# A layer's small product, p times w_pp, moved from the last phases to the start and kept in DRAM between

## The chip, the cores and the metric

One core of one Trainium2 chip runs the whole layer. The metric is the time of one execution in microseconds on the device; the median of three runs stands for the kernel. Matmuls run on TensorE (PE), elementwise work on VectorE (DVE), ScalarE (ACT) and GpSimd (POOL); SyncE (SP) issues most DMAs. Each engine works through its own queue in order.

## The reference, cut to what matters

1024 tokens (x: 1024 x 2048), p: 1024 x 256, all float32. The layer's last part is what the change touches:

```python
u = rmsnorm(h, g_pre)                 # h = x
z = u @ w_in                          # 2048 -> 9216: attention and HGRN2 inputs
...
h = h + rmsnorm(y @ w_out, g_post)    # y: 1024 x 2048
gate = sigmoid(h @ w_pg)              # w_pg: 2048 x 2048
e = p_l @ w_pp                        # p_l: 1024 x 256, w_pp: 256 x 2048
h = h + rmsnorm(gate * e, g_ple)
```

The product e depends on the inputs p and w_pp alone; it is needed first where the gate is ready.

## The kernel before

Every large product is made with float32 operands split in two. K.piece (lines 73 to 87) loads a piece of weights of 128 x 512 (256 KB) on SP into one of three raw buffers, ScalarE casts it to the high part wh (line 83), GpSimd subtracts to the rest wl (line 84), VectorE casts a bfloat16 copy wb (line 85); each of the three has three buffers. A bank of PSUM (128 tokens x 512 columns) takes from each piece three matmuls: high x wh, high x wl, low x wb. So a piece that serves four token tiles feeds 12 matmuls. Four banks are called gb, four others wk. Pieces have a high priority by default, which places their instructions ahead of other ready ones; the order on every engine's queue is fixed ahead, by a planner that works with priorities and program order.

The start: prenorm (line 156) loads x in 8 tiles of 1 MB into five buffers, squares and sums each on ScalarE, scales it on VectorE (line 168), transposes it by 16 small matmuls (tile xp, line 172), and splits it into uh and ul by ScalarE and VectorE (lines 151, 152). Between the tiles lies the first column group of the values, v_group (lines 771 to 786): for token tiles 0 and 1, then 2 and 3, then 4 to 7 (accumulators vb from tile 4 on); its pieces have no high priority, and VectorE makes every other subtract where a piece serves only two token tiles. After that come three more column groups for all tokens, the HGRN2 heads, the attention heads.

The end: y_phase makes y @ w_out for a half of the tokens (512) in four column groups of 512, 16 pieces each; g_phase (line 977) does the same with w_pg and in its sink takes the sigmoid on ScalarE, multiplies it into G (which holds e), squares and sums, and multiplies by the gain. The order is y_phase of half 0, y_phase of half 1, g_phase of half 0, g_phase of half 1; hooks between the pieces do other halves' norms (h_unit, with loads xr of x) and the last additions (final0, with loads hr of hD). G of half 0 lies in the buffer of Y[0], G of half 1 in that of the high part of the first half's h.

The product e in this kernel: e_load loads p of a half, e_unit transposes and splits it (hooks of the phase before), and e_phase (line 971) makes one column group of 512 in two pieces of w_pp, into four banks of wk named pe, and copies each bank into G by ScalarE or VectorE. g_phase calls e_phase twice ahead of column group 0 and twice ahead of group 1. The loop gemm (line 874) runs over the pieces; the last tail pieces are kept until all are there and then worked off token tile by token tile, each followed by its sink.

Of the kernel before, what the change touches and what calls it, by code (L numbers as in the profile page):

```python
# [12 lines left out]
F32 = mybir.dt.float32  # L13
F32R = mybir.dt.float32r
BF16 = mybir.dt.bfloat16
# [8 lines left out]
D = 2048  # L24
INW = 9216
KT = 16
NEG = -1e30
EPS = 1e-6
PLE = 256
NGB = 4  # L30
# [7 lines left out]
def f32(t):  # L38
    return t.bitcast(F32)
# [707 lines left out]
def tile_hybrid(ctx, tc, x, p, positions, w_in, w_out, g_pre, g_post, g_hg, lb_fwd, lb_bwd, w_pg, w_pp, g_ple, out):  # L747
    nc = tc.nc
    K = Kern(tc, ctx)
    x2 = x[0]  # L750
    out2 = out[0]
    w_in = w_in[0]
    w_out = w_out[0]
    w_pg = w_pg[0]
    w_pp = w_pp[0]
    pin = p[0, 0]
# [10 lines left out]
    V = nc.vector  # L767
    vD = [K.dr.tile([S, 512], F32, name=f"vD{i}") for i in range(4)]

    def v_group(cg, toks, pool):  # L770
# [12 lines left out]
        for t in toks:  # L783
            vo = pool.tile([128, 512], F32, name="vo", tag="vo", bufs=3)
            (nc.scalar.copy if t % 2 else V.tensor_copy)(vo, pb[t])
            nc.sync.dma_start(vD[cg][128 * t:128 * t + 128, :], vo)

    with tc.tile_pool(name="p0", bufs=1) as p0:
        warm = K.sp.tile([128, 1], F32, name="warm", bufs=1)
        V.memset(warm, 1.0)  # L790
        nc.scalar.activation(warm, warm, AF.Sqrt)
        K.prenorm(x2, g_pre, p0, (0, 1))
        v_group(0, (0, 1), p0)
        K.prenorm(x2, g_pre, p0, (2, 3))
        v_group(0, (2, 3), p0)
        late = K.prenorm(x2, g_pre, p0, (4, 5, 6, 7))
        v_group(0, (4, 5, 6, 7), p0)
        with tc.issue_after(late[0].ins), tc.issue_after(late[1].ins):
            K.hg_consts((lb_fwd, lb_bwd), g_hg)
        for cg in range(1, 4):  # L800
            v_group(cg, tuple(range(8)), p0)
    with tc.tile_pool(name="big", bufs=1) as big:
# [15 lines left out]
        for n, a in enumerate(heads):  # L818
# [13 lines left out]
            if b:  # L832
# [3 lines left out]
                k = b.keys()  # L836
# [6 lines left out]
    fin = ctx.enter_context(tc.tile_pool(name="fin", bufs=1))  # L843
    Y = [fin.tile([128, 4, D], F32, name=f"Y{i}", tag=f"Y{i}") for i in range(2)]
# [4 lines left out]
    def s2(name):  # L849
        return fin.tile([128, 512], F32, name=name, tag="s2", bufs=3)  # L850
# [3 lines left out]
        nc.sync.dma_start(t, src[0:1, cs].to_broadcast([128, 512]))  # L854
        return t

    def chunk(q):
        return slice(512 * q, 512 * q + 512)
# [7 lines left out]
    def y_load(hf, k):  # L866
        hi, lo = yT[hf]
        with tc.high_priority(offset=PRIO):
# [5 lines left out]
    def gemm(w, act, order, c0, sink, tail, bank, pre=None, get=None):  # L874
        toks = range(4)
        hi, lo = act
        pb = [bank() for t in toks]
        n = len(order)
        pcs = []

        def high(t, k, pc, first):
            a = hi[:, k, 128 * t:128 * t + 128]
            nc.tensor.matmul(pb[t], a, pc[0], start=first, stop=False)  # L883
            nc.tensor.matmul(pb[t], a, pc[1], start=False, stop=False)  # L884

        def low(t, k, pc, last):
            nc.tensor.matmul(pb[t], lo[:, k, 128 * t:128 * t + 128], pc[2], start=False, stop=last)  # L887

        for j, k in enumerate(order):
            if pre:  # L890
                pre(j, k)
            pc = K.piece(w[128 * k:128 * k + 128, c0:c0 + 512], [512], get(j) if get else None)
            if j < n - tail:
                for t in toks:
                    high(t, k, pc, j == 0)
                for t in toks:
                    low(t, k, pc, False)
            else:
                pcs.append((k, pc))
        for t in toks:  # L900
            for i, (k, pc) in enumerate(pcs):
                high(t, k, pc, n == tail and i == 0)
            for i, (k, pc) in enumerate(pcs):
                low(t, k, pc, i == len(pcs) - 1)
            sink(t, pb[t])

    def junk_square(src, acc):
        jk = fin.tile([128, 512], BF16, name="jk", tag="jk", bufs=1)
# [2 lines left out]
    def y_phase(hf, hook):  # L911
        for cg in range(4):
            def sink(t, p):
                dst = Y[hf][:, t, chunk(cg)]
                V.tensor_copy(dst, p)  # L915
                junk_square(dst, yss[hf][:, t, cg:cg + 1])
            gemm(w_out, yT[hf], korder, 512 * cg, sink, 1, K.gb, lambda j, k: hook(cg, j, k))
# [37 lines left out]
        if new:  # L955
            pend.append(new)

    eT = {}

    def e_load(hf, dst):  # L960
        tc.keep_in_program_order(nc.sync.dma_start(dst, pin[512 * hf:512 * hf + 512, :].rearrange("(t p) c -> p t c", p=128)))
        eT[hf] = (dst, fin.tile([128, 2, 512], F32R, name="eh", tag="eh"), fin.tile([128, 2, 512], BF16, name="el", tag="el"))

    def e_unit(hf, t):
        src, eh, el = eT[hf]
        pp = K.wk("pp", (128, 2, 128))
        for k in range(2):
            nc.tensor.transpose(pp[:, k], src[:, t, 128 * k:128 * k + 128], K.ident)
        K.split_evac(eh[:, :, 128 * t:128 * t + 128], el[:, :, 128 * t:128 * t + 128], pp)

    def e_phase(hf, G, cg):
        def sink(t, p):
            (V.tensor_copy if t % 2 else nc.scalar.copy)(G[:, t, chunk(cg)], p)
        gemm(w_pp, eT[hf][1:], [0, 1], 512 * cg, sink, 1, lambda: K.wk("pe"))

    def g_phase(hf, G, hook, fin_t=None, get=None, tail=1):
        for cg in range(4):
            if cg < 2:
                e_phase(hf, G, 2 * cg)
                e_phase(hf, G, 2 * cg + 1)  # L980
            cs = chunk(cg)
# [29 lines left out]
    hT = [half_tiles("t", 0), None]  # L1011
    r0_ = h_rstd(0)

    def every3(f, ext={}, off=0):
        def hook(cg, j, k=None):
            n = 16 * cg + j
            if n % 3 == off and n // 3 < 17:
                f(n // 3)
            if n in ext:
                ext[n]()  # L1020
        return hook

    def e_hooks(hf, dst, n0, n1):
        ext = {n1 + t: (lambda t=t: e_unit(hf, t)) for t in range(4)}
        ext[n0] = lambda: e_load(hf, dst)
        return ext

    y_phase(1, every3(lambda u: h_unit(0, u, r0_), e_hooks(0, Y[1][:, :, 1536:1792], 16, 52)))
    hT[1] = half_tiles("t", 1)
    r1_ = h_rstd(1)  # L1030
    G0 = Y[0]
    ex = f32(hT[1][1][:, 12:16])
# [68 lines left out]
```

## Time and profile before

| | us |
|---|---|
| median of 3 runs | 2865.4 |
| lowest and highest | 2862.57 and 2868.63 |
| the profiled execution, its own time | 2864.4 |
| its span, first to last instruction | 2862.6 |
| TensorE busy | 2733.1 (95%) |
| VectorE busy | 1433.7 (50%) |
| ScalarE busy | 949.0 (33%) |
| GpSimd busy | 1045.1 (37%) |

Busy time is an average over the whole span; what holds the kernel in a stage is read from the stretches, the waits and the timeline of that stage. A matmul's duration in a row covers its pipeline, so consecutive rows overlap; the distance between starts is its cost.

### The profile page before, as it was taken

Reading aid. Unit: us, or ns where it says so; the run is one execution under the profiler, and the core shown is the slowest. Engines: PE = TensorE matmul, PEld = TensorE weight load, DVE = VectorE, ACT = ScalarE, POOL = GpSimd, SP = SyncE. Lnnn points to the kernel's source line nnn. Section 1 sums busy time; section 2 is a strip of 40 time slices with the busy share of each in tenths; the row PEclk is TensorE's granted clock in tenths of the full one; section 3 lists DMA queues with packets and bytes.
Section 4 is the critical chain, followed back from the end, with each engine's and each line's share of the span. In section 5 each row is a group of like instructions: output and inputs, shape, how many; then the busy total and the mean of one; then the engine's idle time right before and its main releaser. Section 6 shows DMA issues by size and latency. Waiting matters only on the chain. (4 is left out here: it accounts for less than half of the span.)

```text
span 2862.6 us, 45162 instructions
## 1 busy us (share of the span) xinstructions
PE 2733.1 (95%) x17104; PEld 1891.4 (66%) x17104; DVE 1433.7 (50%) x3105; ACT 949.0 (33%) x1996; POOL 1045.1 (37%) x833
## 2 busy tenths in 40 slices
PE   6999999999999999999999999999999899999997
PEld 4666666766766766766677667766666566666664
DVE  8601116765365355353655455545655536545445
ACT  5311112222122122122555444545633233333323
POOL 3422223313313313313222232323244554666555
PEclk9999999999999999999999999999999999999998
DMA  6422221211111111114323433343444543443553
GB/s 229 116 65 78 77 85 42 62 54 38 59 45 46 56 45 49 53 41 104 96 81 89 113 86 80 94 107 91 131 132 135 156 144 99 126 122 107 145 151 114
DMA packets 272218, 267.75 MB, mean 94 GB/s; under 512 B 22784, under 2 KB 187648, under 8 KB 270848
## 3 DMA queue, kind: packets, MB, share of 16 engines
q1 hardware_dynamic: 262832, 255.92, 31.0%
q10 hardware_dynamic: 9168, 8.93, 0.9%
q8 instruction: 135, 2.21, 0.3%
q14 instruction: 83, 0.68, 0.1%
HBM read 208.16 MB, written 29.36 MB: 83 GB/s over the span
## 5 line engine op out<-in xcount | busy, mean ns | idle before, releaser
L84 POOL TENSOR_TENSOR wl<-raw,wh 128x512 fp32r<-128x512 f32 x568 | 767.8, 1356 | 1502.9 <-ACT wh L83 1441.2
L85 DVE CAST wb<-raw 128x512 bf16<-128x512 f32 x584 | 401.8, 692 | 806.9 <-PE gb L107 300.0
L83 ACT CAST wh<-raw 128x512 fp32r<-128x512 f32 x584 | 358.4, 617 | 1243.0 <-PE gb L102 395.3
L102 PE MATMUL gb<-uh,wh 128*128 128x512 f32 x1792 | 739.2, 412 | 0.0
L103 PE MATMUL gb<-uh,wl 128*128 128x512 f32 x1792 | 705.4, 394 | 0.0
L107 PE MATMUL gb<-ul,wb 128*128 128x512 bf16 x1792 | 440.0, 383 | 0.0
L102 PEld LDWEIGHTS gb<-uh,wh 128*128 128x128 f32 x1792 | 337.8, 189 | 83.9 <-issue 2.5
L103 PEld LDWEIGHTS gb<-uh,wl 128*128 128x128 f32 x1792 | 337.3, 188 | 68.3
L107 PEld LDWEIGHTS <-wb 128*128 128x128 bf16 x1792 | 156.6, 98 | 205.3 <-issue 54.8
L883 PE MATMUL gb<-wh,yh 128*128 128x512 f32 x512 | 230.6, 450 | 3.9 <-DVE Y L915 3.2
L883 PE MATMUL gb<-wh,th 128*128 128x512 f32 x480 | 214.5, 447 | 0.1
L884 PE MATMUL gb<-wl,yh 128*128 128x512 f32 x512 | 203.0, 397 | 4.1 <-POOL wl L84 4.1
L884 PE MATMUL gb<-wl,th 128*128 128x512 f32 x480 | 189.2, 394 | 3.1 <-POOL wl L84 3.1
L887 PE MATMUL gb<-wb,yl 128*128 128x512 bf16 x512 | 139.3, 386 | 0.0
L657 ACT ACTIVATE asm<-asm,aown 128x256 f32<-128x256 f32 x256 | 127.0, 498 | 25.7 <-DVE aown L654 24.8
L887 PE MATMUL gb<-wb,tl 128*128 128x512 bf16 x480 | 129.0, 382 | 0.0
L883 PEld LDWEIGHTS gb<-wh,yh 128*128 128x128 f32 x512 | 97.7, 191 | 34.1 <-issue 3.2
L778 PE MATMUL gb<-wh,uh 128*128 128x512 f32 x256 | 116.6, 462 | 3.0 <-ACT wh L83 3.0
L884 PEld LDWEIGHTS gb<-wl,yh 128*128 128x128 f32 x512 | 97.3, 190 | 23.6 <-POOL wl L84 4.6
L779 PE MATMUL gb<-wl,uh 128*128 128x512 f32 x256 | 102.3, 406 | 7.9 <-POOL wl L84 5.5
L883 PEld LDWEIGHTS gb<-wh,th 128*128 128x128 f32 x480 | 90.7, 189 | 27.3 <-ACT sg L987 2.2
L884 PEld LDWEIGHTS gb<-wl,th 128*128 128x128 f32 x480 | 90.4, 188 | 22.9 <-POOL wl L84 5.4
(284 smaller groups left out, 3635.8 us busy)
## 6 DMA issues: line engine op xcount, KB each, us to landing
raw<-in_w_in_dram SPq DMA_DIRECT2D x320, 256.0 KB
raw<-in_w_out_dram SPq DMA_DIRECT2D x128, 256.0 KB
raw<-in_w_pg_dram SPq DMA_DIRECT2D x128, 256.0 KB
xt<-in_x_dram SPq DMA_DIRECT2D x8, 1024.0 KB
vD<-vo SPq DMA_DIRECT2D x32, 256.0 KB
aqt<-aqh SPq DMA_DIRECT2D x64, 128.0 KB
aqt<-aq SPq DMA_DIRECT2D x64, 128.0 KB
raw<-yD SPq DMA_DIRECT2D x32, 256.0 KB
```

The costliest lines, as they stand in the source:

```text
L83: nc.scalar.copy(wh, raw)
L84: (sub or nc.gpsimd).tensor_tensor(wl, raw, f32(wh), op=ALU.subtract)
L85: nc.vector.tensor_copy(wb, raw)
L102: nc.tensor.matmul(pb[hf], wh[:, k], self.uh[hf][:, kt], start=(kt == 0), stop=False)
L103: nc.tensor.matmul(pb[hf], wl[:, k], self.uh[hf][:, kt], start=False, stop=False)
L107: mm = nc.tensor.matmul(pb[hf], wb[:, k], self.ul[hf][:, kt], start=False, stop=(kt == KT - 1))
L657: nc.scalar.activation(d, d, AF.Exp, scale=-1.0, bias=own[:, 0, loc, h, i:i + 1], accum_out=own[:, 1, loc, h, i:i + 1])
L778: nc.tensor.matmul(pb[t], hi, wh, start=(k == 0), stop=False)
L779: nc.tensor.matmul(pb[t], hi, wl, start=False, stop=False)
L883: nc.tensor.matmul(pb[t], a, pc[0], start=first, stop=False)
L884: nc.tensor.matmul(pb[t], a, pc[1], start=False, stop=False)
L887: nc.tensor.matmul(pb[t], lo[:, k, 128 * t:128 * t + 128], pc[2], start=False, stop=last)
```

## The change

e_product is called for both halves ahead of prenorm. It loads p, transposes and splits it, makes the four column groups with gemm (both pieces kept until the end: tail 2; banks gb in place of wk) and copies each bank into a staging tile eo, which SP stores to a DRAM tile eD. gemm and chunk are moved up unchanged for it. v_group is defined a second time, the same but for its staging tile vo, which now shares four buffers (tag tA) with eo in place of three of its own; four pairs of DRAM tiles, sD, are named and not used. In the last phases, e_unit, e_phase and the hooks that called them are gone; g_phase begins with e_load, four DMAs on SP that load the half's product from eD into G, 512 columns (1 MB) each. Lines of "..." leave out code that is moved or deleted unchanged.

```diff
@@ in tile_hybrid, ahead of the pool p0 @@
+    def chunk(q):
+        return slice(512 * q, 512 * q + 512)
+
+    def gemm(w, act, order, c0, sink, tail, bank, pre=None, get=None):
...
+        for j, k in enumerate(order):
+            if pre:
+                pre(j, k)
+            pc = K.piece(w[128 * k:128 * k + 128, c0:c0 + 512], [512], get(j) if get else None)
+            if j < n - tail:
...
+            else:
+                pcs.append((k, pc))
+        for t in toks:
+            for i, (k, pc) in enumerate(pcs):
+                high(t, k, pc, n == tail and i == 0)
+            for i, (k, pc) in enumerate(pcs):
+                low(t, k, pc, i == len(pcs) - 1)
+            sink(t, pb[t])
+
+    eD = [K.dr.tile([512, D], F32, name=f"eD{i}") for i in range(2)]
+
+    def e_product(hf, pool, stage):
+        src = pool.tile([128, 4, PLE], F32, name="pr", tag="pr", bufs=2)
+        nc.sync.dma_start(src, pin[512 * hf:512 * hf + 512, :].rearrange("(t p) c -> p t c", p=128))
+        eh = pool.tile([128, 2, 512], F32R, name="eh", tag="eh", bufs=1)
+        el = pool.tile([128, 2, 512], BF16, name="el", tag="el", bufs=1)
+        for t in range(4):
+            pp = K.wk("pp", (128, 2, 128))
+            for k in range(2):
+                nc.tensor.transpose(pp[:, k], src[:, t, 128 * k:128 * k + 128], K.ident)
+            K.split_evac(eh[:, :, 128 * t:128 * t + 128], el[:, :, 128 * t:128 * t + 128], pp)
+        for cg in range(4):
+            def sink(t, p):
+                eo = stage.tile([128, 512], F32, name="eo", tag="tA", bufs=4)
+                (V.tensor_copy if t % 2 else nc.scalar.copy)(eo, p)
+                nc.sync.dma_start(eD[hf][128 * t:128 * t + 128, chunk(cg)], eo)
+            gemm(w_pp, (eh, el), [0, 1], 512 * cg, sink, 2, K.gb)
+
+    def v_group(cg, toks, pool):
...
+            vo = pool.tile([128, 512], F32, name="vo", tag="tA", bufs=4)
...
     with tc.tile_pool(name="p0", bufs=1) as p0:
         warm = K.sp.tile([128, 1], F32, name="warm", bufs=1)
         V.memset(warm, 1.0)
         nc.scalar.activation(warm, warm, AF.Sqrt)
+        e_product(0, p0, p0)
+        e_product(1, p0, p0)
         K.prenorm(x2, g_pre, p0, (0, 1))
@@ the last phases @@
-    eT = {}
-
-    def e_load(hf, dst):
...
-    def e_unit(hf, t):
...
-    def e_phase(hf, G, cg):
-        def sink(t, p):
-            (V.tensor_copy if t % 2 else nc.scalar.copy)(G[:, t, chunk(cg)], p)
-        gemm(w_pp, eT[hf][1:], [0, 1], 512 * cg, sink, 1, lambda: K.wk("pe"))
+    def e_load(hf, G):
+        for cg in range(4):
+            nc.sync.dma_start(G[:, :, chunk(cg)], eD[hf][:, chunk(cg)].rearrange("(t p) c -> p t c", p=128))
 
     def g_phase(hf, G, hook, fin_t=None, get=None, tail=1):
+        e_load(hf, G)
         for cg in range(4):
-            if cg < 2:
-                e_phase(hf, G, 2 * cg)
-                e_phase(hf, G, 2 * cg + 1)
             cs = chunk(cg)
...
-    y_phase(1, every3(lambda u: h_unit(0, u, r0_), e_hooks(0, Y[1][:, :, 1536:1792], 16, 52)))
+    y_phase(1, every3(lambda u: h_unit(0, u, r0_)))
...
-    g_phase(0, G0, every3(lambda u: h_unit(1, u, r1_), e_hooks(1, ex, 17, 28), 2))
+    g_phase(0, G0, every3(lambda u: h_unit(1, u, r1_), 2))
```

## Rows read from the trace of the kernel before

**Rows 1.** The page of the kernel before: busy time by engine with its share of the span, then TensorE (PE) and its granted clock in the 40 slices.
```profile
PE 2733.1 (95%) x17104; PEld 1891.4 (66%) x17104; DVE 1433.7 (50%) x3105; ACT 949.0 (33%) x1996; POOL 1045.1 (37%) x833
...
PE   6999999999999999999999999999999899999997
...
PEclk9999999999999999999999999999999999999998
```

**Rows 2.** Stretches of the start (from : to in us, length, then busy us and instructions (x) of each engine, the granted clock of TensorE, the share of the DMA engines, GB/s).
```profile
0.00:97.89 97.89, 69.63 (x321) 44.96 (x321) 79.05 (x139) 55.05 (x94) 33.23 (x28) 0.97 0.61 207
...
100.00:110.00 10.00, 10.00 (x46) 6.76 (x45) 7.61 (x48) 3.98 (x7) 5.01 (x4) 1.00 0.38 63
```

**Rows 3.** Waits of TensorE in the first 130 us: who waited for whom, us in total, times, longest.
```profile
PE xp L172 <- DVE xt L168: 14.5, 3, 11.5
...
PE gb L779 <- POOL wl L84: 5.5, 4, 2.9
...
PE gb L778 <- ACT wh L83: 3.0, 3, 1.3
```

**Rows 4.** Timeline of the first 25 us: start, us, engine, line, operation, and the idle time before it with its releaser.
```profile
0.74 0.39 SPq L160 DMA_DIRECT2D xt<-in_x_dram  x1
...
2.12 1.65 SPq L76 DMA_DIRECT2D raw<-in_w_in_dram  x3
...
3.81 0.95 SPq L160 DMA_DIRECT2D xt<-in_x_dram  x2
...
5.61 1.91 ACT L166 ACTIVATE xj<-xt 128x2048 bf16<-128x2048 f32 x1 [3.38 <-DMA xt<-in_x_dram]
...
11.54 3.65 PE L172 MATMUL xp<-ident,xt 128*128 128x128 f32 x16 [11.54 <-DVE xt L168]
...
16.46 0.80 PE L778 MATMUL gb<-wh,uh 128*128 128x512 f32 x1 [1.28 <-ACT wh L83]
...
17.79 2.49 SPq L76 DMA_DIRECT2D raw<-in_w_in_dram  x3
...
22.57 1.94 PE L172 MATMUL xp<-ident,xt 128*128 128x128 f32 x16 [1.23 <-DVE xm L118]
```

**Rows 5.** Timeline of TensorE around the four blocks of the product of p (tile pe); gb rows are the gate product behind a block.
```profile
2414.99 0.59 PE L883 MATMUL pe<-wh,eh 128*128 128x512 f32 x1
...
2427.76 0.58 PE L883 MATMUL gb<-wh,th 128*128 128x512 f32 x1
...
2430.49 0.58 PE L883 MATMUL gb<-wh,th 128*128 128x512 f32 x1
...
2475.86 0.58 PE L883 MATMUL pe<-wh,eh 128*128 128x512 f32 x1
...
2490.95 0.58 PE L883 MATMUL gb<-wh,th 128*128 128x512 f32 x1
...
2632.01 0.59 PE L883 MATMUL pe<-wh,eh 128*128 128x512 f32 x1
...
2643.97 0.50 PE L883 MATMUL pe<-wh,eh 128*128 128x512 f32 x1 [3.17 <-DVE G L973]
...
2648.01 0.58 PE L883 MATMUL gb<-wh,th 128*128 128x512 f32 x1
...
2691.70 0.59 PE L883 MATMUL pe<-wh,eh 128*128 128x512 f32 x1
...
2707.97 0.58 PE L883 MATMUL gb<-wh,th 128*128 128x512 f32 x1
```

**Rows 6.** Instructions on the tiles xp (transposes of x), gb (accumulators, first 140 us) and vb (accumulators of token tiles 4 to 7): duration in ns min/median/max, first and last start.
```profile
L172 PE MATMUL xp<-ident,xt x128: 270/273/444, 11.5 to 97.7; 128*128 128x128 f32 x128
...
L778 PE MATMUL gb<-wh,uh x64: 389/541/988, 16.5 to 90.7; 128*128 128x512 f32 x64
...
L778 PE MATMUL vb<-wh,uh x256: 387/389/586, 97.9 to 398.7; 128*128 128x512 f32 x128
```

**Rows 7.** Groups by line in the first 130 us (busy us, mean ns | idle before), then two casts from the timeline, the second beside a subtract on GpSimd that ran from 55.69 to 57.01 us.
```profile
L84 POOL TENSOR_TENSOR wl<-raw,wh 128x512 fp32r<-128x512 f32 x30 | 46.4, 1553 | 81.2 <-ACT wh L83 62.5 <-PE gb L779 7.0 <-PE gb L782 6.3
...
L85 DVE CAST wb<-raw 128x512 bf16<-128x512 f32 x46 | 30.9, 691 | 14.8 <-PE vb L782 8.3 <-DMA raw<-in_w_in_dram 4.9 <-PE gb L782 1.7
...
L152 DVE TENSOR_TENSOR ul<-xp,uh 128x512 bf16<-128x512 f32 x32 | 20.4, 681 | 2.4 <-ACT uh L151 2.4
...
L168 DVE SCALAR_TENSOR_TENSOR xt<-xt,xr,gpre 128x2048 f32<-128x2048 f32 x8 | 18.8, 2349 | 0.1
...
11.99 0.43 DVE L85 CAST wb<-raw 128x512 bf16<-128x512 f32 x1 [0.25 <-DMA raw<-in_w_in_dram]
...
55.69 1.32 POOL L84 TENSOR_TENSOR wl<-raw,wh 128x512 fp32r<-128x512 f32 x1 [2.55 <-PE gb L782]
...
55.78 1.51 DVE L85 CAST wb<-raw 128x512 bf16<-128x512 f32 x1
```

**Rows 8.** What the DMA engines moved in 40 slices of the first 110 us (2.75 us each); a stretch of the gate phase with a join of two column groups and no product of p in it; one piece of the chain that ended last; the longest wait of ScalarE's cast from 2180 us on.
```profile
GB/s 48 411 426 405 432 423 70 234 268 349 238 255 310 145 154 252 260 196 0 215 136 211 123 259 10 118 182 87 13 162 116 201 143 180 163 168 5 116 85 26
...
2550.00:2600.00 50.00, 49.51 (x228) 32.67 (x227) 27.16 (x32) 18.47 (x35) 36.88 (x28) 1.00 0.42 118
...
2556.00 3.42 DMA xr<-in_x_dram
...
ACT wh L83 <- PE gb L883: 146.9, 85, 8.6
```

More of the change, by code (lines that the diff above doesn't have):

```diff
@@ L786, in v_group, with high, low @@
             nc.sync.dma_start(vD[cg][128 * t:128 * t + 128, :], vo)
+    def chunk(q):
+        return slice(512 * q, 512 * q + 512)
+    def gemm(w, act, order, c0, sink, tail, bank, pre=None, get=None):
+        toks = range(4)
+        hi, lo = act
+        pb = [bank() for t in toks]
+        n = len(order)
+        pcs = []
+        def high(t, k, pc, first):
+            a = hi[:, k, 128 * t:128 * t + 128]
+            nc.tensor.matmul(pb[t], a, pc[0], start=first, stop=False)
+            nc.tensor.matmul(pb[t], a, pc[1], start=False, stop=False)
+        def low(t, k, pc, last):
+            nc.tensor.matmul(pb[t], lo[:, k, 128 * t:128 * t + 128], pc[2], start=False, stop=last)
+        for j, k in enumerate(order):
[4 more added lines that the diff above has]
+                for t in toks:
+                    high(t, k, pc, j == 0)
+                for t in toks:
+                    low(t, k, pc, False)
+            else:
+                pcs.append((k, pc))
+        for t in toks:
+            for i, (k, pc) in enumerate(pcs):
[3 more added lines that the diff above has]
+            sink(t, pb[t])
@@ new lines, in v_group @@
+    def v_group(cg, toks, pool):
+        c0 = (2048, 2560, 7168, 7680)[cg]
+        pb = {t: (K.gb() if t < NGB else K.wk("vb")) for t in toks}
+        for k in range(KT):
+            wh, wl, wb = K.piece(w_in[128 * k:128 * k + 128, c0:c0 + 512], [512], prio=False,
+                                 sub=V if len(toks) == 2 and k % 2 else None)
+            for t in toks:
+                hi = K.uh[t // 4][:, k, 128 * (t % 4):128 * (t % 4) + 128]
+                nc.tensor.matmul(pb[t], hi, wh, start=(k == 0), stop=False)
+                nc.tensor.matmul(pb[t], hi, wl, start=False, stop=False)
+            for t in toks:
+                lo = K.ul[t // 4][:, k, 128 * (t % 4):128 * (t % 4) + 128]
+                nc.tensor.matmul(pb[t], lo, wb, start=False, stop=(k == KT - 1))
+        for t in toks:
+            vo = pool.tile([128, 512], F32, name="vo", tag="tA", bufs=4)
+            (nc.scalar.copy if t % 2 else V.tensor_copy)(vo, pb[t])
+            nc.sync.dma_start(vD[cg][128 * t:128 * t + 128, :], vo)
@@ L788, in tile_hybrid @@
+    sD = [(K.dr.tile([128, 8, 512], F32, name=f"sh{i}"), K.dr.tile([128, 8, 512], BF16, name=f"sl{i}")) for i in range(4)]
     with tc.tile_pool(name="p0", bufs=1) as p0:
@@ L855, in g2 @@
         return t
-    def chunk(q):
-        return slice(512 * q, 512 * q + 512)
     def half_tiles(name, hf):
@@ L872, in y_load @@
             V.tensor_tensor(lo[:, k], raw, f32(hi[:, k]), op=ALU.subtract)
[L874 to L905, printed above, removed]
     def junk_square(src, acc):
@@ L1012, in tile_hybrid, with every3 @@
     r0_ = h_rstd(0)
-    def every3(f, ext={}, off=0):
+    def every3(f, off=0):
         def hook(cg, j, k=None):
@@ L1018, in hook @@
                 f(n // 3)
-            if n in ext:
-                ext[n]()
-        return hook
[L1023 to L1026, printed above, removed]
-    y_phase(1, every3(lambda u: h_unit(0, u, r0_), e_hooks(0, Y[1][:, :, 1536:1792], 16, 52)))
+        return hook
+    y_phase(1, every3(lambda u: h_unit(0, u, r0_)))
     hT[1] = half_tiles("t", 1)
@@ L1031, in tile_hybrid @@
     G0 = Y[0]
-    ex = f32(hT[1][1][:, 12:16])
-    g_phase(0, G0, every3(lambda u: h_unit(1, u, r1_), e_hooks(1, ex, 17, 28), 2))
+    g_phase(0, G0, every3(lambda u: h_unit(1, u, r1_), 2))
     gs = K.sp.tile([128, 4], F32, name="gst4")
```

7 lines of the change are left out of this document (removed).

## Prediction

> **What bounds the kernel now.** I read the page first: TensorE is busy 95% of the span, and only the first and the last of the forty slices fall short of it [rows 1]. So time is won only by taking work off TensorE or by filling its idle time, and the first slice holds much of that. Next, the stretches of the start by window: until 97.9 us TensorE is busy 69.6 us, VectorE 79 us; from 100 us on TensorE has no gap [rows 2]. The waits of TensorE there name VectorE's scaling of x (14.5 us, of which 11.5 ahead of the first instruction) and the weight conversion [rows 3]. The timeline shows the cause: x tile 0, issued at 0.74, is squared from 5.61, TensorE's first transpose comes at 11.54 and its first matmul at 16.46 [rows 4].
>
> **A measure of the start.** A piece of weights feeds 12 matmuls to four banks; undisturbed they take 2430.49 - 2427.76 = 2.73 us [rows 5]. Sixteen transposes take 1.94 us [rows 4]. Up to 97.9 us, where the first matmul into a vb bank starts, TensorE has done 128 transposes and 64 triples, that is 192 matmuls [rows 6]: 8 x 1.94 + 16 x 2.73 = 59.2 us undisturbed. The start thus wastes 97.9 - 59.2 = 38.7 us, 11.5 before the first transpose and 27.2 after it, at half speed or idle.
>
> **What the change removes.** The product of p is made in eight column groups, four to a half of the tokens; they lie in four blocks of two, and nothing else runs on TensorE in them. From a block's first matmul to the first one behind it: 2427.76 - 2414.99 = 12.77, 2490.95 - 2475.86 = 15.09, 2648.01 - 2632.01 = 16.00, 2707.97 - 2691.70 = 16.27 us [rows 5], together 60.1 us. Eight groups of two pieces are 16 x 2.73 = 43.7 us undisturbed, so 16.4 us of the blocks were waits for evacuation and conversion, or half speed. The 16 transposes of p (1.9 us) go too: 62.0 us. Not all of that is won. Part of the waits belongs to the join of two phases (VectorE's chain for the norm and the sigmoid evacuations), and stays without the product. A join without a product inside lies in the stretch from 2550 to 2600 us, with 0.5 us idle [rows 8]; the worst wait in a block is 3.17 us [rows 5]. For four joins that is 2 to 13 us; I take r = 4, nearer to the join that looks like the new ones.
>
> **What it adds at the start.** The same 43.7 + 1.9 = 45.6 us of TensorE, plus what the start wastes then, U. Only U decides whether moving pays. Its terms:
> - First matmul. p is half of an x tile, which took 4.9 us to land [rows 4]; its transposes, split and weight pieces stand behind. Bounds 5 us and today's 11.5; I take 7.5, since VectorE's 2.35 us scaling and the gain row aren't in this path.
> - Half speed. The first matmul of the start takes 0.80 us [rows 4], where 0.39 to 0.58 is usual [rows 5]. Bounds 0 and 4 us; I take 1.5.
> - Eight column groups of two pieces each with three buffers for converted pieces: the second piece of a group waits for a buffer that the previous group frees only with its last bank, then ScalarE, GpSimd (1.55 us here) and VectorE convert [rows 7]. The late blocks had the same ring: (12.77 - 10.92)/2 = 0.9 to (16.27 - 10.92)/2 = 2.7 us a group, mean 2.05. Here both pieces are now held to the end (tail 2), and prenorm's ScalarE and VectorE instructions stand between. Bounds 7 and 32 us; I take the mean, 16.4.
> - The rest of today's 27.2 us. While the product runs (45.6 + 16.4 + 9 = some 71 us), VectorE owes it 16 casts of 0.69, 16 evacuations of some 0.68 (a split of that size) and 8 splits of half the size, 25 us. A prenorm tile costs VectorE 2.35 + 4 x 0.68 + about 1 = 6 us [rows 7], so 46 us remain, up to seven tiles; five x buffers and FIFO order allow some five or six. I leave 8 us; bounds 3 and 27.
> U = 7.5 + 1.5 + 16.4 + 8 = 33 us, against 38.7 now. VectorE's total, 79 + 25 = 104 us, against a stage of 45.6 + 59.2 + 33 = 138, is no bound.
>
> **The queues.** SP now issues two p loads, sixteen w_pp pieces and 32 stores (8.4 MB) ahead of or among the x loads. Each store waits for an evacuation, and x tiles and weight pieces are queued behind it. What waits there: prenorm on ScalarE, hence TensorE's transposes. Today SP put four x tiles, the gain and three pieces into the queue by 4.8 us, and then stood until 17.79 for a free raw buffer [rows 4]. A piece issued at about 3 us behind 3 MB landed at 11.9 [rows 4, 7], so pieces behind x tiles come late. Product, x and gain together are 8.4 + 4.2 + 1.0 + 8.4 + 1.0 = 23 MB; at the first slices' 426 GB/s that is 54 us, at 250 (later slices) 92 us [rows 8], both inside 138 us: covered in sum, and a starved ring is in the bound of 32. GpSimd's 16 subtracts (25 us) lie beside 33 us in 97.9 [rows 2].
>
> **The late loads.** Each half reads its product back in four 1 MB loads on SP. The first half's target is free well before; the second's waits for the last matmul of the first gate phase, and behind it on SP stand w_pg pieces and hr loads. Moving at 118 GB/s with a share of 0.42 is 281 GB/s in full [rows 8], so 4.2 MB in one burst delay a piece behind them by 15 us. The pieces have slack: ScalarE's casts mostly wait for TensorE to free a buffer (146.9 us), so three raw and two converted pieces lie ready, some 4 x 2.73 = 11 us. An xr load already costs 3.42 us of the chain, with GpSimd's subtracts behind it [rows 8]. Bounds 0 and 15 us a half; I take 1 each, L = 2, as SP waits for raw buffers between the loads. The sums of the sink need the first chunk a whole column group later, 16 x 2.73 = 43.7 us: free. Nothing, too, for the DRAM tiles that nobody uses, and for vo's move to four buffers shared with eo: TensorE waits for no vo [rows 3]; should the eo stores land late, evacuations and banks wait for them, which is in the bound of 32.
>
> **Sum.** 45.6 - 62.0 + r + L + (U - 38.7) = U + L + r - 55.1. With 33 + 2 + 4: -16 us. The profiled execution takes 2864.4 us, 1.0 below the median of 2865.4: 2848.4 there, 2849 for the median.
>
> **A rule of the skill.** A cast of 128x512 takes 0.43 us alone and 1.51 us when it meets a subtract on GpSimd [rows 7]. The Trainium skill, "SBUF — State Buffer", section "Who interferes with whom", says that VectorE and GpSimd share one pair of ports as an exclusive lock, the later one blocked for the whole instruction. The trace agrees: that cast ended only after the subtract beside it. It speaks against the change: the sixteen moved pieces come where VectorE is fullest, and by the lock up to 16 x 1.1 = 17 us more would stand in VectorE's queue. This doesn't break the sum (121 of 138 us), but a blocked cast holds up prenorm and evacuation behind it; for it I give rival D 0.10 where I would give 0.05.
>
> **The rivals.**
> - B, better: prenorm hides wholly and a group wastes 0.9 us: U = 7.5 + 1.5 + 7 + 4 = 20, sum -55.1 + 20 + 6 = -29, 2836. For: TensorE no longer waits for x first. Against: the late blocks reached 0.9 only once of four. 0.18.
> - C, it doesn't do what it says: the planner puts prenorm behind the product, so that most of the 27.2 us remain, 24 say, as the x tiles are there by then: U = 7.5 + 1.5 + 16.4 + 24 = 49, sum 0, 2865. For: x loads are now later in program order and w_pp pieces carry the high priority. Against: SP stands idle in the rows and has x buffers free. 0.14.
> - D, slower: the ring of three paces the product, each group waiting behind a 1.91 us square on ScalarE, a 2.35 us scaling on VectorE or a blocked subtract. With j us a group the sum is 9 + 8j + 8 + 6 - 55.1 = 8j - 32: nothing won from j = 4, 5.7 us lost from j = 4.7; at j = 5 it is +8, 2873. For: rows with 3.17 us waits in the late blocks, with less prenorm about. Against: their mean is 2.05. 0.10.
> - E: the read-back comes in bursts and starves pieces, xr or hr: 7 us a half makes -4, 2861; the full 15 makes +12. 0.08.
>
> **How the numbers follow.** The forecast, -24 to -8, has 0.50. Its own range is 2841 to 2857; for 8 in 10 it takes in B (down to 2831), C and the near side of D (up to 2868). A measurement of this kernel can tell some 0.2%, 5.7 us. Faster: 0.50 + 0.18 + 0.05 of C and E = 0.73; within: 0.16, C, half of E, the near side of D; slower: 0.11, D and the ends of C and E.
>
> **What will show it.** The first matmul before 9 us and its operands p and w_pp; groups of the product that take 5.5 us plus about 2; the first vb matmul at 97.9 + 45.6 - 5.7 = 138 us (110 to 130 speaks for B, over 150 for C or D); no block of pe in the gate phases and joins under 2 us; ScalarE's casts not waiting for w_pg longer than now. Wrong it would be if SP held the x loads behind stores, or if the late end does not come nearer by 55 us or more.

## The result: slower by 0.4%

The changed kernel takes 2878.39 us (median of 4 runs, 2876.84 to 2880.80), the kernel before 2865.69 us beside it (4 runs): ratio 1.0042, 95% interval 1.0030 to 1.0054, some 12 us slower where 16 us faster were forecast. The profiled execution of after takes 2877.27 us with a span of 2875.5 us; that of before has a span of 2862.6 us. So 12.9 us are to be found between the two traces.

The start of each phase on TensorE (first matmul of it, by tile) shows where:

| phase starts | before | after | after - before | forecast |
|---|---|---|---|---|
| first v matmul into a vb bank | 97.9 | 147.4 | +49.5 | +39.9 |
| first matmul behind the v blocks (L102) | 400.7 | 452.9 | +52.2 | |
| first matmul of the y phase (yh) | 2010.5 | 2065.5 | +55.0 | +39.9 |
| first gate matmul (th) | 2427.8 | 2473.4 | +45.6 | |
| first matmul on wx, in the last column group | 2817.8 | 2829.9 | +12.1 | -16 |
| end of the span | 2862.6 | 2875.5 | +12.9 | -16 |

The start lost 9.6 us more than forecast, the phases from yh to wx gave back 42.9 us instead of 56, and 5.5 us came between, where nothing was changed.

The page of after, TensorE's lines [rows 1 has those of before]: the busy share is the same; the short slices are the first (7 tenths busy, 6 before), the second and the last.

```profile
PE 2739.2 (95%) x17104; PEld 1894.2 (66%) x17104; DVE 1443.0 (50%) x3105; ACT 948.3 (33%) x1996; POOL 1045.4 (36%) x833
...
PE   7899999999999999999999999999999999999997
...
PEclk9999999999999999999999999999999999999998
```

**The start.** Two tables of after: stretches (columns as in [rows 2]), cut where the product ends, and TensorE's waits of the first 150 us, which answer to [rows 3].

```profile
0.00:74.00 74.00, 54.20 (x240) 34.40 (x241) 50.94 (x81) 36.78 (x64) 26.76 (x26) 1.00 0.84 279
74.00:147.40 73.40, 62.83 (x290) 39.50 (x289) 58.71 (x99) 39.18 (x71) 27.41 (x18) 0.95 0.60 185
```

```profile
PE pp L834 <- POOL ident masks.py:199: 9.4, 1, 9.4
PE gb L801 <- POOL wl L84: 4.2, 4, 1.7
PE gb L852 <- POOL wl L84: 3.6, 5, 1.3
PE gb L852 <- DVE wl L84: 3.3, 3, 2.5
PE xp L172 <- DVE ul L152: 2.0, 1, 2.0
PE gb L800 <- ACT eh L151: 2.0, 1, 2.0
PE gb L800 <- ACT eo L839: 1.8, 1, 1.8
PE gb L800 <- DVE xt L121: 1.3, 1, 1.3
```

The 14.5 us for which x had kept TensorE waiting [rows 3] are gone; x costs 2.0 us now. In their place stand 9.4 us ahead of p's transposes and some 10 us inside the product. The order on TensorE, by tile (first and last start), is: product, then x.

```profile
L804 PE MATMUL gb<-wb,el x64: 379/389/650, 12.8 to 72.7; 128*128 128x512 bf16 x64
...
L172 PE MATMUL xp<-ident,xt x128: 272/273/477, 46.6 to 147.4; 128*128 128x128 f32 x128
...
L851 PE MATMUL gb<-wh,uh x64: 387/481/988, 74.0 to 137.6; 128*128 128x512 f32 x64
```

Against [rows 6], where the first x transpose came at 11.5 us and the first v matmul at 16.5 us, they now come at 46.6 and 74.0 us. The 9.4 us have a cause that no row of before hinted at. Timeline of after:

```profile
7.63 1.44 POOL L84 TENSOR_TENSOR wl<-raw,wh 128x512 fp32r<-128x512 f32 x1
9.03 0.29 POOL masks.py:199 TENSOR_SCALAR_AFFINE_SELECT ident<-ident 128x128 f32<-128x128 f32 x1
...
9.37 1.97 PE L834 MATMUL pp<-ident,pr 128*128 128x128 f32 x8 [9.37 <-POOL ident masks.py:199]
10.99 0.78 PE L800 MATMUL gb<-wh,eh 128*128 128x512 f32 x1
```

The identity that every transpose uses is finished on GpSimd; the subtractions for the first w_pp pieces carry the planner's high priority and were put ahead of it. In before, its last step ran at 1.08 us.

The x tiles did go out late, which the prediction had named as a sign of being wrong: SP issued the fifth at 45.60 us, right behind four stores. TensorE waited only 2.0 us for x all the same.

**The late phases.** TensorE's waits in the gate phases (first th to first wx), before and then after:

```profile
PE pe L883 <- DVE G L973: 5.1, 2, 3.2
PE gb L884 <- POOL wl L84: 3.1, 4, 1.5
PE pe L883 <- ACT G L973: 1.8, 2, 0.9
PE pe L883 <- DVE Y L973: 1.7, 1, 1.7
PE hp L949 <- POOL Y L941: 1.6, 1, 1.6
PE pe L883 <- ACT Y L973: 0.2, 1, 0.2
```

```profile
PE gb L801 <- POOL wl L84: 9.6, 5, 4.9
PE hp L991 <- POOL Y L983: 1.5, 1, 1.5
PE gb L800 <- ACT wh L83: 1.0, 1, 1.0
PE gb L804 <- DVE wb L85: 0.9, 2, 0.5
```

The 8.8 us on pe are gone with the product, and the waits of the gate product for its weights grew from 3.1 to 9.6 us (L884 of before is L801 of after): 13.5 us in all before, 13.0 us after. The sum stayed, under other names. The whole stretch from yh to wx says the same (columns as in [rows 2]; before, then after): TensorE's idle time, the length less its busy time, is 31.0 and 32.9 us.

```profile
2010.50:2817.80 807.30, 776.34 (x3539) 507.05 (x3537) 432.61 (x603) 287.25 (x568) 443.82 (x331) 0.99 0.45 130
```

```profile
2065.50:2829.90 764.40, 731.47 (x3329) 478.49 (x3328) 408.58 (x563) 265.28 (x528) 423.27 (x315) 0.98 0.49 142
```

The largest wait, in the timeline of after:

```profile
2487.77 5.09 SPq L76 DMA_DIRECT2D raw<-in_w_pg_dram  x2
...
2496.37 0.90 SPq L981 DMA_DIRECT2D xr<-in_x_dram  x2
...
2501.27 2.48 POOL L983 TENSOR_TENSOR Y<-Y,xr 128x512 f32<-128x512 f32 x2 [6.99 <-DMA xr<-in_x_dram]
...
2503.71 3.91 POOL L84 TENSOR_TENSOR wl<-raw,wh 128x512 fp32r<-128x512 f32 x3
...
2505.20 0.80 PE L801 MATMUL gb<-wl,th 128*128 128x512 f32 x1 [4.91 <-POOL wl L84]
2505.80 0.63 PE L800 MATMUL gb<-wh,th 128*128 128x512 f32 x1
```

GpSimd stood 6.99 us for xr with the next subtraction of weights behind it, TensorE 4.91 us for that subtraction, and its next matmuls took 0.63 us instead of 0.39. GpSimd had waited for xr before the change too; its waits in the gate phases, before and then after:

```profile
POOL Y L941 <- DMA xr<-in_x_dram: 22.8, 7, 4.7
```

```profile
POOL Y L983 <- DMA xr<-in_x_dram: 16.2, 5, 7.0
```

### The profile page after: what moved, and what is told of

Same layout as the page of the kernel before. It is cut to its first block, busy times and chain, and to the rows that moved or that the text cites. A ratio compares the mean times of both kernels' runs of the same rounds, so it can differ in the third digit from the quotient of the medians.

```text
span 2875.5 us, 45257 instructions
## 1 busy us (share of the span) xinstructions
PE 2739.2 (95%) x17104; PEld 1894.2 (66%) x17104; DVE 1443.0 (50%) x3105; ACT 948.3 (33%) x1996; POOL 1045.4 (36%) x833
## 3 DMA queue, kind: packets, MB, share of 16 engines
q1 hardware_dynamic: 271664, 272.70, 32.9%
## 4 chain that ended last, share of the span: by engine, by line
PE 74%; DVE 10%; DMA 7%; issue 3%; POOL 3%; ACT 1%; SPq 1%; ACTq 0%; DVEq 0%; POOLq 0%
PE gb L103 12%; PE gb L102 12%; PE gb L107 12%; PE gb L800 6%; PE gb L801 6%; PE gb L804 5%; PE asc L645 2%; PE apt L702 2%; PE vb L851 2%; PE vb L852 2%; PE vb L855 2%; DVE Q L282 2%; PE gb L852 2%; PE gb L851 2%; DVE wb L85 1%
## 5 line engine op out<-in xcount | busy, mean ns | idle before, releaser
L102 PE MATMUL gb<-uh,wh 128*128 128x512 f32 x1792 | 738.8, 412 | 0.0
L102 PEld LDWEIGHTS gb<-uh,wh 128*128 128x128 f32 x1792 | 337.4, 188 | 83.5 <-issue 1.4
L801 PE MATMUL gb<-wl,yh 128*128 128x512 f32 x512 | 204.0, 399 | 5.1 <-POOL wl L84 5.1
L801 PE MATMUL gb<-wl,th 128*128 128x512 f32 x480 | 191.7, 399 | 9.9 <-POOL wl L84 9.6
L801 PEld LDWEIGHTS gb<-wl,yh 128*128 128x128 f32 x512 | 97.6, 191 | 25.2 <-POOL wl L84 6.3
L801 PEld LDWEIGHTS gb<-wl,th 128*128 128x128 f32 x480 | 91.5, 191 | 31.1 <-POOL wl L84 13.8
```

The costliest lines, as they stand in the source:

```text
L102: nc.tensor.matmul(pb[hf], wh[:, k], self.uh[hf][:, kt], start=(kt == 0), stop=False)
```

## The experiments

Ratios are against the kernel before on the same chip in the same job, with 95% intervals. The phase starts named (vb, L102, yh, th, wx) are those of the table above.

**1. The late half alone.** The product is left out; the late loads read rows of x in its place.

```diff
-        e_product(0, p0, p0)
-        e_product(1, p0, p0)
...
-            nc.sync.dma_start(G[:, :, chunk(cg)], eD[hf][:, chunk(cg)]...)
+            nc.sync.dma_start(G[:, :, chunk(cg)], x2[512 * hf:512 * hf + 512, chunk(cg)]...)
```

> The late half of the change alone: the product p w_pp is left out, and the four loads of a half read x in its place (same size and layout), so the start is that of the kernel before. Theory 1 (the waits in the late blocks belong to the joins of the phases and stay when the product goes): the gate phases keep some 21 us of waste, the late end comes 40 to 46 us nearer than before, about 2822 us. Rival (the forecast: the waits are the product's and go with it): 54 to 58 us nearer, about 2810 us.

Measured: 2815.86 us, ratio 0.9838 (0.9821 to 0.9855), about -46 us. TensorE's waits in its gate phases:

```profile
PE gb L801 <- POOL wl L84: 11.3, 8, 5.1
PE hp L989 <- POOL Y L981: 1.5, 1, 1.5
PE gb L804 <- DVE wb L85: 1.0, 2, 0.5
PE gb L800 <- ACT sg L1011: 0.9, 1, 0.9
```

With no product anywhere, 14.9 us of waits are there all the same. From yh to wx it takes 761.7 us, before 807.3: 45.6 us less, about the product's undisturbed time. That the two agree to the tenth is chance: in run 7, which leaves these phases as they were, the stretch takes 803.6 us. TensorE's idle time in it is 32.1 us:

```profile
2007.70:2769.40 761.70, 729.63 (x3330) 477.64 (x3329) 405.60 (x563) 265.11 (x528) 422.63 (x315) 0.99 0.47 142
```

The waits around the product did not go with it. This run has the eight late loads, with other rows, so it does not show what these cost.

**2. The start half alone.** Product made and stored at the start, and made again late, as before; the stored copy is not read. Against before, and without the definitions that the calls need:

```diff
+        e_product(0, p0, p0)
+        e_product(1, p0, p0)
```

> The early half alone: the product is made and stored at the start, and made again in the last phases as in the kernel before, where its stored copy is not read. Theory 1 (the waste of the start stays, the product adds its own time): first vb matmul at 147 us as in the changed kernel, total 50 to 56 us over the kernel before, about 2919 us. Forecast: 40 us over, 2906 us. If the middle of the kernel is later by more than the start is, that is a cost of the early half (its tiles, its plan); if not, the late loads make it.

Measured: 2918.29 us, ratio 1.0194 (1.0178 to 1.0209), about +56 us; first vb matmul 148.8 us. The two halves add up within their intervals: -46 + 56 = +10, against +12 measured for both. So there is no sign of an effect that needs both halves.

**3. No stores.** Product made at the start, its 32 stores left out, late loads from x.

```diff
-                nc.sync.dma_start(eD[hf][128 * t:128 * t + 128, chunk(cg)], eo)
```

> The changed kernel without the 32 stores of the product; the late loads read x in its place, so what is left out is that the product reaches the gate. Theory 2 (the 8.4 MB of stores, their waits on SP and on the staging buffers hold the start): first vb matmul from 147 to 135 us or earlier, total 2866 us or less. Theory 1 (the plan's order and VectorE set the start, the DMA engines do not): under 4 us, first vb matmul at 143 us or later, total 2874 us or more.

Measured: 2868.37 us, ratio 1.0023 (1.0012 to 1.0035) beside 1.0042 for after; first vb matmul 143.1 us beside 147.4. The stores cost some 5 us. The total lies between the two ranges expected, the vb start in the range of theory 1 (143 us or later). What the loads cost on the same queue is not shown by this run.

**4. x ahead of p on the load queue.**

```diff
-            nc.sync.dma_start(xt, x[128 * t:128 * t + 128, :])
+            with self.tc.high_priority(offset=2 * PRIO):
+                nc.sync.dma_start(xt, x[128 * t:128 * t + 128, :])
```

> The changed kernel with the loads of x and of the gain at the highest priority, so that they lead on SP. Theory 3 (x is held on SP behind waiting pieces and stores, so prenorm can't run under the product): the fifth x tile is issued before 20 us instead of 45.6, first vb matmul 10 us or more earlier than 147 us, total 2868 us or less. Theory 1 with the planner's order (transposes of x are queued behind the product on TensorE whatever the loads do): within 4 us, 2875 to 2882 us.

Measured: 2881.67 us, ratio 1.0071 (1.0050 to 1.0092). Five x tiles were issued by 3.9 us, yet the first x transpose came at 85.1 us, behind a product that now waited for p until 22.7 us. Early x loads alone do not help while the product stands ahead of x on TensorE; the total is in the range of theory 1.

**5 to 8. Order on TensorE, and the size of the first v block.** "Order" calls the product behind the prenorm of tiles 0 and 1, its w_pp pieces without priority. "Merge" gives the first v block all eight token tiles at once, 16 pieces of weights instead of 48; "before, merged" is the control without the change. "Filler" does both, with half of the product behind tile 1 and half behind tile 4. The edits of order (without those that lower the priority), then of merge:

```diff
+        K.prenorm(x2, g_pre, p0, (0, 1))
         e_product(0, p0, p0)
         e_product(1, p0, p0)
-        K.prenorm(x2, g_pre, p0, (0, 1))
```

```diff
-        K.prenorm(x2, g_pre, p0, (0, 1))
-        v_group(0, (0, 1), p0)
-        K.prenorm(x2, g_pre, p0, (2, 3))
-        v_group(0, (2, 3), p0)
-        late = K.prenorm(x2, g_pre, p0, (4, 5, 6, 7))
-        v_group(0, (4, 5, 6, 7), p0)
+        late = K.prenorm(x2, g_pre, p0, tuple(range(8)))
+        v_group(0, tuple(range(8)), p0)
```

> The changed kernel, but with the product called behind the prenorm of the first two token tiles, and with the loads and conversions of w_pp at ordinary priority. Everything is still computed. Theory 1 (the cost is the place: in the changed kernel all 64 column-group joins of the product stand on TensorE's queue ahead of the first transpose of x, at 46.6 us, so the prenorm of the first tiles, 11.5 to 16 us in the kernel before, no longer covers anything): the first x transposes go back to near 12 us, some of the eight prenorms run beside the product, the last column of vb starts near 130 to 140 us instead of 147.4, total 2862 to 2872 beside 2878 for the changed kernel. Theory 2 (the v block that follows costs its 74 to 76 us for 59.2 us of matmuls however it is entered, because it is split in 48 pieces whose conversion paces it): the total stays within 4 us of the changed kernel's 2878.

> The changed kernel, but the first block of the v columns goes over all eight token tiles at once, with 16 pieces of weights instead of 48 (the prenorm of all eight tiles before it). Everything is still computed. Theory 1 (order): the product no longer needs the two-tile split as cover, the prenorms of the later tiles run beside the product, but their transposes stay behind it; the v block falls from about 76 to about 63 us, total some 8 to 14 us under the changed kernel, 2864 to 2870. Theory 2 (48 pieces pace the block): the same sign, as much as the 16.4 us that the block takes over its matmuls, total 2860 to 2866. If neither is at work (the start is held by the DMAs of x and weights): within 4 us of the changed kernel.

> Control for the run above: the kernel before with the same first block over all eight token tiles at once, and no product early. Everything is computed. Here nothing fills TensorE while the tiles of x arrive, so theory 1 expects the first block to wait for the last prenorm (near 45 us) and to end later than 97.9 us, at about 107 us: total 2870 to 2878, slower than the kernel before. Theory 2 (the pieces pace the block whatever stands beside it) expects that 32 pieces fewer give back at least the 16 us: total 2850 to 2858.

> The changed kernel with both: the two halves of the product stand between prenorms (behind tiles 0 and 1, and behind tile 4), w_pp at ordinary priority, and the first v block goes over all eight token tiles at once. Everything is still computed. Theory 1: the product then is work that covers the prenorm, which was its point; the unused time of the start falls from 42.6 us to 15 to 25 us, total 2852 to 2862, below both kernels. Theory 2 (the pieces alone): no better than the run with the merged block alone. Theory 3 (the start is held by what VectorE, ScalarE and the DMAs must do for x and the weights, 79 and 55 busy us of the first 98 in the kernel before): the end of the start stays at 140 us or later and the total at 2866 or above.

Measured, with TensorE's idle time ahead of three kinds of work up to the first L102 matmul (the groups by line of the first 460 us, summed; for before, [rows 3] shows the larger of the waits):

| kernel | us | ratio | idle: product | x transposes | v blocks | first L102 |
|---|---|---|---|---|---|---|
| before | | 1 | | 16.6 | 11.6 | 400.7 |
| after | 2878.39 | 1.0042 (1.0030, 1.0054) | 19.8 | 2.0 | 10.7 | 452.9 |
| order | 2877.66 | 1.0061 (1.0046, 1.0076) | 5.4 | 21.1 | 9.5 | 456.9 |
| merge | 2856.86 | 0.9991 (0.9980, 1.0001) | 19.3 | 2.4 | 4.6 | 440.0 |
| before, merged | 2854.17 | 0.9977 (0.9967, 0.9986) | | 24.9 | 1.1 | 393.9 |
| filler | 2868.64 | 1.0031 (1.0016, 1.0045) | 7.4 | 21.9 | 4.8 | 450.2 |

Three of those groups, x and product in "order", then the product in "merge":

```profile
L172 PE MATMUL xp<-ident,xt 128*128 128x128 f32 x128 | 21.9, 329 | 21.1 <-DVE xt L168 11.5 <-DVE xm L118 8.4 <-DVE ul L152 1.2
...
L801 PE MATMUL gb<-wl,eh 128*128 128x512 f32 x64 | 26.8, 419 | 2.7 <-POOL wl L84 2.3 <-DMA eD<-eo 0.5
```

```profile
L800 PE MATMUL gb<-wh,eh 128*128 128x512 f32 x64 | 31.4, 494 | 5.0 <-ACT eo L839 2.1 <-ACT eh L151 1.8 <-DVE eo L839 1.0
...
L834 PE MATMUL pp<-ident,pr 128*128 128x128 f32 x16 | 3.3, 348 | 9.0 <-POOL ident masks.py:199 9.0
```

The theory of order falls: with x first, x again waits 21.1 us and the product 5.4; with the product first, 2.0 and 19.8. Whoever stands first on TensorE pays some 20 us (17 to 25 in the table), because nothing is there yet to fill them, and the next one pays 2 to 7 us. What helps with or without the change is the merged block; even the control, for which the theory of order expected a slower kernel, gains 7 us. So the v block's waits, by name those for the conversion of its pieces, go with 32 of the 48 pieces. The same edit also moves six prenorms ahead of the block; no run separates the two. In none of the orders tried does the product hide anything: from "before, merged" to "merge" the first L102 matmul moves by 46.1 us, for 45.6 us of product. "Filler" came out where its third theory had it, 2866 us or above; that VectorE, ScalarE and the DMA engines hold the start, the reason given there, is not isolated by any run.

**9 to 12. Repairs at the start, wider rings late.** The identity made ahead (on "merge"); larger rings for xr and the gain rows (on after); all of it with eight result tiles; and the kernel before with merge and rings.

```diff
-        make_identity(nc, self.ident)
+        with tc.high_priority(offset=2 * PRIO):
+            make_identity(nc, self.ident)
```

```diff
-        return fin.tile([128, 512], F32, name=name, tag="s2", bufs=3)
+        return fin.tile([128, 512], F32, name=name, tag="s2", bufs=4)
...
-        t = fin.tile([128, 512], F32, name="g2", tag="g2", bufs=2)
+        t = fin.tile([128, 512], F32, name="g2", tag="g2", bufs=3)
```

> The merged-block kernel, with the making of the identity matrix put ahead of all else by priority. Everything is computed. Theory (the product's transposes, first at 9.0 us there, wait only for GpSimd's last step of the identity at 8.64 us, which stands behind three subtractions for w_pp): they start at 5 to 7 us, when p has landed, and the first x transposes and everything behind come 2 to 4 us earlier: total 2853 to 2855 beside 2857. Rival (the first matmul waits for the converted w_pp pieces or for TensorE's clock anyway): the transposes move, the first x transposes do not, total within 1 us.

> The changed kernel with more tiles for the two rings that the late phases share: four for xr, sg and hr instead of three, three for the broadcast rows of g_post and g_ple instead of two. Everything is computed. Theory (the waits of the late blocks, which the changed kernel kept, come from xr loads that stand on the load queue behind a g_ple load that waits for its tile: GpSimd's addition waited 7.0 us at 2501, the subtraction for the next piece behind it, TensorE 4.9 us): the 4.9 us wait goes, and the unused time between the first th matmul and the first wx matmul falls from 21 us to 14 to 17 us, total 2871 to 2875. Rival (the phase joins themselves, whose chains of statistics and conversions are as long as before, make the waits): 21 us stay, total 2876 to 2880.

> All that the runs so far point to, with the product made ahead: the merged first block, the identity ahead, eight tiles instead of four for the results of the product and of the v blocks on their way to DRAM, and the larger rings of the late phases. Everything is computed. If the parts add up (merge 20 us by the run, identity 2 to 4, result tiles about 4, late rings 4 to 7), total 2842 to 2850. If only the merged block counts: 2855 to 2858.

> Control for the run above: the kernel before, with its product in the late phases, the merged first block and the same larger rings of the late phases. Everything is computed. Theory that the product costs at the start what it gives late, in whatever order (start +46, late -46): 2845 to 2852, within 6 us of the run above. If the product made ahead does pay once nothing is in its way at the start: the run above is more than 6 us faster than this one.

Measured: identity ahead 2863.88 us, ratio 1.0006 (0.9997 to 1.0016); rings 2871.94, 1.0033 (1.0021 to 1.0045); all 2860.40, 0.9994 (0.9983 to 1.0005); before with merge and rings 2854.60, 0.9979 (0.9967 to 0.9990). The identity bought 1.1 us at once, since p's landing is next (7.9 us), and x transposes came 3.2 us earlier, at 45.4; then TensorE waited 7.9 us among them for VectorE's splits, and the first L102 matmul came at 443.7, later than the 440.0 of "merge"; the ratio is no better than that of "merge" (0.9991), where 2 to 4 us had been expected. The rings did nothing that shows in the gate phases (355.5 us against 356.5). All repairs together, expected at 2842 to 2850 us, miss that by 10 us and do not beat "merge" by itself: the parts do not add up. Their control, before with merge and rings, is 6 us faster than they are (expected 2845 to 2852). Timeline of the run with larger rings: xr still goes out behind a w_pg load that waits for its tile.

```profile
2490.01 4.55 SPq L76 DMA_DIRECT2D raw<-in_w_pg_dram  x2
2494.59 0.91 SPq L981 DMA_DIRECT2D xr<-in_x_dram  x2
...
2499.02 2.48 POOL L983 TENSOR_TENSOR Y<-Y,xr 128x512 f32<-128x512 f32 x2 [6.90 <-DMA xr<-in_x_dram]
...
2502.95 0.79 PE L801 MATMUL gb<-wl,th 128*128 128x512 f32 x1 [4.33 <-POOL wl L84]
```

**13 to 15. xr on ScalarE's queue**, in after, in "merge" and in "before, merged".

```diff
-            tc.keep_in_program_order(nc.sync.dma_start(xt, x2[r0:r0 + 128, cs]))
+            tc.keep_in_program_order(nc.scalar.dma_start(xt, x2[r0:r0 + 128, cs]))
```

> The changed kernel with the sixteen xr loads of each half issued from ScalarE's queue instead of SP's, so that they stand behind no weight load. Everything is computed. Theory (queue order: xr stands behind a w_pg load that waits for a tile which a subtraction frees that stands behind the addition of xr): GpSimd's waits for xr fall from 16 us to under 6 us, the 4.9 us wait of TensorE at 2505 goes, the gate phase shortens from 356.5 us to 348 to 352 us, total 2869 to 2874. Rival (the join makes the waits, whatever the queue): 355 to 358 us, total 2876 to 2880.

> The same with the merged first v block. Everything is computed. If both repairs hold and add up: 2849 to 2853; if only the merged block counts: 2855 to 2860.

> Control: the kernel before (product in the late phases) with the merged first v block and xr on ScalarE's queue. Everything is computed. Theory (the late product sits in the joins and covers part of their waits already, so that the repair is worth less here): 2850 to 2855, level with or behind the run above. If the place of the product still decides, with a start that cannot hide it: 2846 to 2850, ahead of the run above.

Measured: 2858.24 us, ratio 0.9988 (0.9979 to 0.9998); 2849.33, 0.9949 (0.9932 to 0.9966); 2847.01, 0.9948 (0.9932 to 0.9964). Waits of GpSimd, then of TensorE, in the gate phases of the first of them:

```profile
POOL Y L983 <- DMA xr<-in_x_dram: 8.9, 5, 2.6
```

```profile
PE gb L804 <- DVE wb L85: 3.6, 3, 1.9
PE hp L991 <- POOL Y L983: 2.7, 1, 2.7
PE gb L801 <- POOL wl L84: 2.5, 5, 0.8
PE gb L800 <- ACT sg L1013: 0.7, 1, 0.7
```

GpSimd's waits for xr fall from 16.2 to 8.9 us in all (under 6 was expected) and the longest from 7.0 to 2.6 us; TensorE's waits for the subtraction fall from 9.6 to 2.5 us, while 3.6 us for VectorE's cast come up behind them (13.0 to 9.5 in all). The gate phases take 352.0 us instead of 356.5, and the y phase ahead of them (first yh to first th), which the expectation did not reckon with, 397.6 instead of 407.9: 14.8 us less in two phases, and some 15 us in all by the ratios, more than expected. The last two runs put the question of the change once more, with both stretches repaired: the product early makes L102 come 48.8 us later (442.3 against 393.5) and the stretch from yh to wx 44.3 us shorter (751.1 against 795.4), and the times cannot be told apart. Both beat both kernels.

## Why the prediction was wrong

The sum was U + L + r - 55.1, with U = 33, L = 2, r = 4. Measured in the same way:

- **r, the waits that stay with the joins: 4 forecast, and with L 6; together 19.1 measured.** This step failed most, 13.1 of the 29 us between forecast and result. The 62.0 us of the late blocks were put down as 45.6 of work and 16.4 of waits, and I let 12.4 of the waits go with the product, by the one join without a product that I had looked at, a join of two column groups inside a phase [rows 8]. The phases from yh to wx gave back 42.9 us in after and 45.6 in run 1: about the work, and none of the waits. Both have the late loads in them, so no run separates r from L. Run 13 shows the cause of a part of the waits, xr behind a weight load on one queue: from yh to wx TensorE's idle time falls from 32.9 to 22.7 us. The cause of the rest stays open. That in before the late product was work that covered such waits fits the rows (GpSimd waited 22.8 us for xr in the gate phases, TensorE 3.1 for the subtraction), but it is argued: the repair shortens the stretch from yh to wx by 8.8 us with the product early (runs 6 and 14) and by 8.2 with the product late (runs 7 and 15).
- **"The rest of today's 27.2 us": 8 forecast, 18.1 measured.** This is the second failed step. From 74.0 to 147.4 us after does what is left of the start, 59.2 - 3.9 (two tiles' transposes come earlier) = 55.3 us of work in 73.4 us. I took the 27.2 us for prenorm that the product would cover. It did cover most of the prenorm: 2.0 us of waits for x are left. But of the 10.6 us idle some 8 were ahead of the v block's weights, and 7.5 us more were slower matmuls (62.83 - 55.3). The granted clock of the stretch is 0.95 in the mean: 0.70 from 100 to 105 us, behind a wait of 2.5 us for weights, and 0.76 from 145 to 150 us, behind the 2.0 us for x. Waits for weights stood in the trace of before too, as 11.6 of 28.2 us, 8.5 of them in [rows 3]. The merged block (runs 6 and 7) takes most of the waits inside the v blocks away, 10.7 to 4.6 us with the change and 11.6 to 1.1 without.
- **The rest of U: 25.4 forecast, 24.5 measured.** Up to 74.0 us: 9.4 idle ahead of p's transposes, 10.4 idle inside the product, 4.7 slower matmuls (54.20 - 49.5). The sum came right by luck, for its parts were off both ways. The first term was too small (7.5): p did not wait for itself but for the identity on GpSimd. Half speed was too small (1.5), the column groups too dear (16.4). The 2.05 us a group of the late blocks held slow matmuls too; counted alike, it was (10.4 + 4.7)/8 = 1.9 us a group here. Rival D, a ring that paces the product at 4 us a group or more, is out by the same number. The exclusive lock of VectorE's and GpSimd's ports, which the Trainium skill ("SBUF — State Buffer", "Who interferes with whom") states and for which I had raised D, did not decide here. The casts did get longer, 1.42 us in the median up to 74 us where 0.43 is the time of one alone, but no wait of TensorE inside the product names them.
- **L: 2 forecast, not measured by itself.** Run 1 makes the same loads of other rows, so the 2.7 us from it to after (761.7 to 764.4 from yh to wx) are not their cost; before and run 7 differ by 3.7 us in that stretch with nothing changed in it. The loads of the first half came spread out, from 2323 to 2430 us; those of the second came within 16 us, from 2670.7 to 2686.6, and from 2660 to 2720 us TensorE waited 2.2 us in all. So rival E, 7 us or more a half, finds no support. Stores were not costed apart; run 3 puts them at some 5 us.
- **Rival C** described the order rightly (product wholly ahead of x) and its time, 2865, lay nearer than mine. Most of the 27.2 us did remain (18.1; it had 24), but not for its reason: run 5 changes that order and gains nothing.
- **The middle**, which I took as unmoved, cost 5.5 us. From vb to L102 it was 2.7 us, 2.1 of them waits for result tiles (run 2 has 1.7, run 11 with eight tiles none); the prediction had put vo's move to shared tiles at nothing. From L102 to yh it was 2.8 us. In the other runs that last stretch took 1606.6 to 1612.6 us with no order that I can see; its cause stays open.
- **A reading:** the page of before has a third short slice, the 32nd (8 tenths) [rows 1], which the prediction passed over. It bears on no term.

Put together: 49.5 - 42.9 + 2.7 + 2.8 + 0.8 at the very end = 12.9 us. In plain words, the product of p is 45.6 us of TensorE in either place. Much of TensorE's idle time at the start is the time until the first operands are ready, and a product with operands of its own to load, split and convert did not fill it in any order tried; put first, it becomes the one that waits.

## What to carry to other kernels

Work moved into idle time fills it only if it is ready sooner than what the engine waits for; count its own loads, conversions and setup, down to a shared constant such as the identity, before the gain. Waits seen next to a step need not belong to it: leave the step out (one run) before counting them as won. And where an in-order engine adds a loaded tile, try that load on a queue on which no load stands that waits for the same engine; here it was worth 8 to 15 us.

## What the runs showed of the hardware that I had not expected

The granted clock in the rows is 1.00, the 2.4 GHz level, for the stretch from 0 to 74 us of after, and also for the few us that hold its first matmuls (columns as in [rows 2]):

```profile
9.40:13.00 3.60, 3.60 (x13) 2.88 (x14) 1.27 (x3) 2.43 (x4) 0.11 (x2) 1.00 0.99 337
```

Yet these matmuls, behind an idle start, took 0.63 to 0.78 us where 0.39 is usual: the clock of a stretch does not show every slow spell in it. With the product at the start the DMA engines moved 279 GB/s at a share of 0.84 up to 74 us, and taking 8.4 MB of stores away, which brought the share to 0.53, was worth only some 5 us: the high DMA share there was not the bound.
